# FFN up-projection pairs as Strassen's seven products, with the down units of one chunk between the products of the next

## The chip, the cores and the metric

One core of one Trainium2 chip runs the whole program. The metric is the device time of one execution in microseconds. PE is TensorE (matmul), DVE VectorE, ACT ScalarE, POOL GpSimd, SP SyncE, which here issues the loads of weights.

## What is computed

One step of a two-layer encoder on 576 tokens: 512 of a prompt and 64 of a sample. Layer 0 mixes with attention and a linear recurrence, layer 1 with chunked spatial gating. Each mixer and each FFN is followed by x <- LN(alpha x + f(x)) over 1024 features. The change lies in the gated FFN of both layers:

```
def conv_ffn(x, conv_state, w_up, conv_w, conv_b, w_down):
    hc, new_state = causal_dwconv(x @ w_up, conv_state, conv_w, conv_b)   # width 3, along the tokens
    g, u = jnp.split(hc, 2, axis=-1)
    return (jax.nn.gelu(g) * u) @ w_down, new_state
```

`w_up` is 1024 x 5632 (g and u of 2816 each, 22 tiles of 128), `w_down` 2816 x 1024, all float32.

## The kernel before

**Layout.** x lies feature-major: 8 tiles of 128 features by 576 tokens, worked on in two halves of 288 (`HALF`). Every large product is made of float32r parts, each operand split exactly into high and low. `triplet` (L288) issues three matmuls for one inner tile of 128: high by high (L293), high by low of the activations (L294), low by high (L295). The normalised x is held as `xh` and `xl`, the hidden tiles as `hh` and `hl`.

**Weight stream.** `units` lists all weight tiles in order of use. `dma_next` (L134 to L143) has SP load one into one of four `raw` buffers, at most four ahead of the splits. A split (`split_part`, L162) is an ACT copy to the high part (L164) and a DVE subtraction for the low part (L165), into one of two sets of four slots, A and B.

**FFN before** (`ffn`, L1039). The 22 column pairs are worked through in three chunks of 8, 7 and 7 (`CHUNKS`). Per pair j there are two up units, g and u: 8 inner tiles x 3 matmuls x 2 halves = 48 matmuls each. `up_post` evacuates the banks on ACT (L1056, L1058, L1059), POOL makes the base of the convolution (L1062), DVE its other two taps (L1064), then gelu on ACT (L1069), multiply on DVE (L1074) and the split of the hidden tile (`h_split`, L801 on ACT, L802 on DVE). After a chunk come its eight down units, which add into x (`z_post`, L1095, L1097). The first four up units of an FFN run one half of the tokens after the other (`first_group`), while the layer norm of the second half is still made by hooks at fixed places in the first half's sweep: statistics (L422 on PE, L432 a power on POOL), broadcast (L439), centering, scaling (L462 on POOL) and low parts (L471 on DVE).

**Order.** Each engine takes its instructions in program order. The DMAs of SP and POOL stand in these orders too. What is issued early in the code is early on its engine, whether its inputs are there or not.

Of the kernel before, what the change touches and what calls it, by code (L numbers as in the profile page):

```python
# [25 lines left out]
D = 1024  # L26
# [13 lines left out]
CHUNKS = ((0, 8), (8, 15), (15, 22))  # L40
# [7 lines left out]
class Unit:  # L48
    def __init__(self, src, slot, nk, width=128):
        self.src, self.slot, self.nk, self.width = src, slot, nk, width  # L50
        self.raw = self.hi = self.lo = None
        self.parts = ((0, nk),)


@with_exitstack
def stream_step(ctx, tc, I, O):
# [21 lines left out]
    units = []  # L78

    def wunit(w, off, ncols, c0, k0, nk, slot):  # L80
        u = Unit(dram(w, off + k0 * 128 * ncols + c0, [[ncols, 128], [128 * ncols, nk], [1, 128]]), slot, nk)
        units.append(u)
        return u

    def vunit(w, ncols, c0, k0, slot, width=512):
        u = Unit(dram(w, k0 * 128 * ncols + c0, [[ncols, 128], [128 * ncols, 2], [1, width]]), slot, 2, width)
        units.append(u)
        return u

    def weight_list():  # L90
# [11 lines left out]
        def ffn_units(layer):  # L102
            n = 0
            up, down = {}, {}
            for c, (j0, j1) in enumerate(CHUNKS):
                for j in range(j0, j1):
                    for s in range(2):
                        up[j, s] = wunit(I["ffn_w_up"], layer * D * 2 * DFF, 2 * DFF, s * DFF + 128 * j, 0, 8,
                                         "BA"[(n // 4) % 2])
                        n += 1  # L110
                for m in range(8):
                    down[c, m] = wunit(I["ffn_w_down"], layer * DFF * D, D, 128 * m, j0, j1 - j0,
                                       "BA"[(n // 4) % 2])
                    n += 1
            Fs.append((up, down))
# [15 lines left out]
    st = {"dma": 0, "split": 0}  # L131
    live = {"A": 0, "B": 0}

    def dma_next():  # L134
        if st["dma"] >= len(units) or st["dma"] >= st["split"] + 4:
            return False
        u = units[st["dma"]]
        st["dma"] += 1
        u.raw = raws.tile([128, 1040], FT, name="raw")
        for k0, k1 in u.parts:  # L140
            nc.sync.dma_start(u.raw[:, k0 * u.width:k1 * u.width].rearrange("p (k c) -> p k c", k=k1 - k0),
                              u.src[:, k0:k1])
        return True  # L143

    def split_next():
        if st["split"] >= st["dma"]:
            return False
        u = units[st["split"]]
        p = wpool[u.slot]
        if p is None or live[u.slot] >= 4:  # L150
            return False
        st["split"] += 1
# [1217 lines left out]
```

## Time and profile before

| | |
|---|---|
| three timed executions | 1321.57, 1319.81, 1320.72 us (median 1320.72) |
| span of the profiled execution | 1319.8 us |
| PE, DVE, ACT, POOL busy | 98%, 58%, 37%, 30% of the span |
| mean granted clock of PE | 0.987 |
| matmuls | 9567 |
| DMA | 113.8 MB, mean 86 GB/s |

The profile is one execution; the page gives no time for it other than its span, which lies 0.9 us under the median of the timed ones. A busy share is a mean over the whole program, and an engine that is half idle can still be the one that another waits for at a given place.

### The profile page before, as it was taken

The page shows a single profiled execution, that of the slowest core. Times are in us where ns is not written, and L with a number is a line of the kernel's source. Part 1 is how long each engine was busy: PE and PEld are TensorE (multiplying, and loading weights), DVE is VectorE, ACT ScalarE, POOL GpSimd, SP SyncE. Part 2 cuts the span into 40 slices and gives each one's busy share as a digit, 9 for nine tenths or more (in the row PEclk, how much of TensorE's full clock was granted, in tenths as well). Part 3 has the DMA queues.
Part 4 walks back from the last instruction along what each step waited for, and adds up shares of the span by engine and source line. Part 5 has one row for each costly group of instructions (what it writes and reads, how often), then busy time and mean ns, then how long its engine had stood idle before and what let it go on. Part 6 is the DMA issues. An engine that isn't in the chain of part 4 may idle for free. (4 is left out here: it accounts for less than half of the span.)

```text
span 1319.8 us, 23538 instructions
## 1 busy us (share of the span) xinstructions
PE 1290.8 (98%) x9567; PEld 1256.0 (95%) x9567; DVE 768.4 (58%) x1294; ACT 483.1 (37%) x936; POOL 398.2 (30%) x603
## 2 busy tenths in 40 slices
PE   8999999999999999999999998999999999999995
PEld 8999888999999999999999788999999999999995
DVE  4557777777543555355564348777653465445556
ACT  4553554445421332234334242444431233223331
POOL 3322222763200221022183025565320122012234
PEclk9999999999999999999999998999999999999997
DMA  9316221314232223322312412314323222322112
GB/s 234 113 33 199 79 84 41 97 47 144 83 96 80 74 74 94 97 75 71 94 38 68 139 50 73 96 33 128 113 80 96 78 66 81 97 86 64 43 36 72
DMA packets 192017, 113.80 MB, mean 86 GB/s; under 512 B 4221, under 2 KB 184733, under 8 KB 191909
## 3 DMA queue, kind: packets, MB, share of 16 engines
q1 hardware_dynamic: 191300, 111.95, 28.9%
q8 instruction: 75, 1.23, 0.4%
q0 software_dynamic: 608, 0.35, 0.2%
q14 instruction: 34, 0.27, 0.1%
HBM read 107.07 MB, written 5.22 MB: 85 GB/s over the span
## 5 line engine op out<-in xcount | busy, mean ns | idle before, releaser
L293 PE MATMUL mm<-xh,whiA 128*128 128x288 f32 (+2 forms) x960 | 285.4, 297 | 1.6 <-ACT xh L512 1.6
L295 PE MATMUL mm<-xh,wloA 128*128 128x288 f32 (+2 forms) x960 | 283.7, 296 | 1.4 <-DVE wloA L165 1.4
L294 PE MATMUL mm<-xl,whiA 128*128 128x288 f32 (+2 forms) x960 | 283.9, 296 | 0.5 <-DVE xl L513 0.5
L1064 DVE SCALAR_TENSOR_TENSOR y<-hb,vecF,y 128x578 f32<-128x578 f32 x176 | 146.5, 834 | 193.3 <-POOL y L1062 190.2
L1062 POOL TENSOR_SCALAR y<-hb,vecF 128x578 f32<-128x578 f32 x88 | 81.6, 928 | 557.5 <-issue 546.2
L293 PE MATMUL mm<-xh,whiB 128*128 128x288 f32 x768 | 226.5, 295 | 0.0
L295 PE MATMUL mm<-xh,wloB 128*128 128x288 f32 x768 | 226.4, 295 | 0.0
L294 PE MATMUL mm<-xl,whiB 128*128 128x288 f32 x768 | 226.2, 295 | 0.0
L165 DVE TENSOR_TENSOR wloA<-raw,whiA 128x1024 fp32r<-128x1024 f32 (+3 forms) x118 | 141.3, 1211 | 110.4 <-ACT whiA L164 109.8
L293 PEld LDWEIGHTS mm<-xh,whiA 128*128 128x128 f32 x960 | 181.3, 189 | 2.5 <-ACT xh L512 1.8
L295 PEld LDWEIGHTS mm<-xh,wloA 128*128 128x128 f32 x960 | 181.1, 189 | 1.6 <-DVE wloA L165 1.6
L294 PEld LDWEIGHTS mm<-xl,whiA 128*128 128x128 f32 x960 | 181.2, 189 | 0.7 <-DVE xl L513 0.7
L293 PE MATMUL mm<-hh,whiA 128*128 128x288 f32 (+2 forms) x576 | 171.5, 298 | 0.1
L294 PE MATMUL mm<-hl,whiA 128*128 128x288 f32 (+2 forms) x576 | 170.4, 296 | 0.8 <-DVE hl L1202 0.7
L295 PE MATMUL mm<-hh,wloA 128*128 128x288 f32 (+2 forms) x576 | 170.0, 295 | 0.0
L164 ACT ACTIVATE whiA<-raw 128x1024 fp32r<-128x1024 f32 (+3 forms) x118 | 119.5, 1025 | 133.7 <-PE mm L294 81.4
L293 PEld LDWEIGHTS mm<-xh,whiB 128*128 128x128 f32 x768 | 144.1, 188 | 0.0
L294 PEld LDWEIGHTS mm<-xl,whiB 128*128 128x128 f32 x768 | 144.1, 188 | 0.0
L295 PEld LDWEIGHTS mm<-xh,wloB 128*128 128x128 f32 x768 | 144.1, 188 | 0.0
L294 PEld LDWEIGHTS mm<-hl,whiA 128*128 128x128 f32 x576 | 108.8, 189 | 1.2 <-DVE hl L1202 1.2
L293 PEld LDWEIGHTS mm<-hh,whiA 128*128 128x128 f32 x576 | 108.8, 189 | 0.4 <-DVE x L361 0.4
L295 PEld LDWEIGHTS mm<-hh,wloA 128*128 128x128 f32 x576 | 108.6, 189 | 0.0
(330 smaller groups left out, 2374.1 us busy)
## 6 DMA issues: line engine op xcount, KB each, us to landing
raw<-in_ffn_w_up_dram SPq DMA_DIRECT2D x88, 512.0 KB
raw<-in_ffn_w_down_dram SPq DMA_DIRECT2D x32, 448.0 KB
raw<-in_ffn_w_down_dram SPq DMA_DIRECT2D x16, 512.0 KB
raw<-in_w_in_o_dram SPq DMA_DIRECT2D x16, 512.0 KB
raw<-in_w_in_e_dram SPq DMA_DIRECT2D x14, 512.0 KB
raw<-in_w_out_e_dram SPq DMA_DIRECT2D x8, 512.0 KB
raw<-in_w_out_o_dram SPq DMA_DIRECT2D x8, 512.0 KB
biasb<-nbd SPq DMA_DIRECT2D x4, 832.0 KB
```

Source lines behind the costliest of these rows:

```text
L164: ACT.activation(u.hi[:, c], u.raw[:, c], AF.Copy)
L165: DVE.tensor_sub(u.lo[:, c], u.raw[:, c], u.hi[:, c])
L293: PE.matmul(o, wh, h[:, k, a:b], start=first, stop=False)
L294: PE.matmul(o, wh, l[:, k, a:b], start=False, stop=False)
L295: PE.matmul(o, wl, h[:, k, a:b], start=False, stop=last)
L1062: POOL.tensor_scalar(y, t[:, 2:580], V[:, 88 + ct:89 + ct], V[:, 132 + ct:133 + ct], op0=OP.mult, op1=OP.add)
L1064: DVE.scalar_tensor_tensor(y, t[:, q:q + 578], V[:, 44 * q + ct:44 * q + ct + 1], y, op0=OP.mult, op1=OP.add)
```

## The change

The FFN of both layers is rewritten. The pairs j = 0 and 1 stay plain. From j = 2 on, g and u of a pair are one 2x2 block product: the inner dimension in two halves of 512, the columns g and u, the tokens in two halves of 288. Strassen's form in seven products of 12 matmuls (4 inner tiles x 3) takes the place of eight, so 84 matmuls for a pair instead of 96, 20 pairs per layer. In exchange there are sums of operands: of weights, per pair (`pair_sums` on POOL; `pair_split` copies the sum to a high part and its negative, on ACT, and an accumulating DMA from POOL's queue adds the sum to the latter, which leaves the low part), of x, once per FFN (`x_sums`, `x_sum3`, `x_split3`), and of products, per pair on DVE.

`CHUNKS` becomes seven (2, 3, 3, 3, 3, 3 and 5 tiles). Hidden tiles live in a ring of five. The eight down units of a chunk run inside the windows of the next chunk: `window` issues the seven products with two or three calls of `d_run` after or between them, while the convolution, gelu and split of the pair before (`pend`) and the weights of the pair after (`nxt`) are made. A window at a chunk's start has two units, the next two have three, the last two of an FFN none. Down weights come through one buffer `draw`, loaded by SP and split one unit ahead. The base of the convolution moves from POOL to ACT. For the FFN's start the weight sums of pair 2 are issued inside the first half's sweep, before the hooks of the layer norm. The last chunk's down units and the final layer norm are put in another order (`ffn_tail`, `fin_early`).

```diff
-CHUNKS = ((0, 8), (8, 15), (15, 22))
+CHUNKS = ((0, 2), (2, 5), (5, 8), (8, 11), (11, 14), (14, 17), (17, 22))
+RING = 5
...
+    BL = {"B11": (0, 0), "B21": (4, 0), "B22": (4, H2), "t3": (0, H2)}
...
+            def base(self, s):
+                ct = s * NJ + self.j
+                ACT.activation(self.y[s], self.t[s][:, 2:580], AF.Identity, scale=V[:, 88 + ct:89 + ct],
+                               bias=V[:, 132 + ct:133 + ct])
...
+        def x_sums():
+            for e in range(2):
+                lo, hi = x[:, 2 * e:2 * e + 2], x[:, 4 + 2 * e:6 + 2 * e]
+                s = tmp[e].raw[:, :2 * H2].rearrange("p (k c) -> p k c", k=2)
+                for name, eng, a, b in (("t1", DVE, lo[:, :, H2:], lo[:, :, :H2]), ("t2", DVE, hi[:, :, H2:], s),
+                                        ("t4", POOL, s, hi[:, :, :H2])):
+                    eng.tensor_sub(s, a, b)
+                    ACT.activation(tb[name, 0][e], s, AF.Copy)
+                    DVE.tensor_sub(tb[name, 1][e], s, tb[name, 0][e])
...
+        def prod(bk, w, off, name):
+            hi, lo = w
+            o = bk[:, :H2]
+            for k in range(4):
+                c = slice(off + 128 * k, off + 128 * k + 128)
+                PE.matmul(o, hi[:, c], operand(name, 0, k), start=k == 0, stop=False)
+                PE.matmul(o, hi[:, c], operand(name, 1, k), start=False, stop=False)
+                PE.matmul(o, lo[:, c], operand(name, 0, k), start=False, stop=k == 3)
...
+        def pair_sums(g):
+            r1, r2 = g.one.raw, g.two.raw
+            POOL.tensor_add(r2[:, b_], r2[:, a_], r2[:, b_])
+            POOL.tensor_sub(r2[:, a_], r1[:, a_], r2[:, a_])
+            POOL.tensor_sub(r1[:, a_], r2[:, b_], r1[:, a_])
+            POOL.tensor_sub(r1[:, b_], r1[:, b_], r1[:, a_])
+
+        def pair_split(g, i):
+            hi, lo = (t[:, :1024] for t in g.w[i])
+            r = (g.two if i == 2 else g.one).raw[:, :1024]
+            ACT.activation(hi, r, AF.Copy)
+            ACT.activation(lo, r, AF.Copy, scale=-1.0)
+            POOL.dma_start(lo, r, accum_op=OP.add)
+            if i == 3:
+                free_raw(2)
...
+        def d_split():
+            i = dn["split"]
+            if i < dn["load"] and i < dn["run"] + 2:
+                dn["split"] += 1
+                u = down[dq[i]]
+                u.hi, u.lo = (t[:, 512:512 + u.nk * 128] for t in S[i % 2][1])
+                ACT.activation(u.hi, draw[:, :u.nk * 128], AF.Copy)
+                DVE.tensor_sub(u.lo, draw[:, :u.nk * 128], u.hi)
+                d_load()
...
+        def window(g, nxt, pend, nd, first):
...
+            prod(b1, w1, 0, "B11")
+            ACT.activation(p1, b1[:, :H2], AF.Copy)
+            if nxt:
+                pair_hi(nxt)
+            pend.conv(1)
+            pend.conv(0)
+            b0 = mmbank()
+            prod(b0, w1, 512, "B21")
+            if nxt:
+                pair_lo(nxt, 1)
+            DVE.tensor_add(me.t[0][:, 2:2 + H2], b0[:, :H2], p1)
+            if nxt:
+                pair_lo(nxt, 0)
+            pend.gelu()
+            pend.mul()
+            pend.split()
+            if nxt:
+                pair_sums(nxt)
+            b5 = mmbank()
+            prod(b5, w2, 0, "t4")
+            if nd > 2:
+                d_run()
+            if nxt:
+                pair_split(nxt, 2)
+            b4 = mmbank()
+            prod(b4, w3, 512, "t1")
+            b3 = mmbank()
+            prod(b3, w3, 0, "t3")
+            if nd > 2:
+                d_run()
+            if nxt:
+                pair_split(nxt, 3)
+            b2 = mmbank()
+            prod(b2, w4, 0, "t2")
+            DVE.tensor_add(u2, b2[:, :H2], p1)
...
+            prod(b6, w4, 512, "B22")
...
+            for _ in range(1 if nd > 2 else nd):
+                d_run()
...
+            hooks = prev.hooks(1, (13, 15, 17, 20))
...
+            hooks[2] = begin
+            hooks[5] = lambda: pair_sums(g)
+            hooks[8] = lambda: pair_split(g, 2)
+            hooks[11] = lambda: pair_split(g, 3)
+            sweep(us, 0, xh, xl, post, outer=True, hooks=hooks)
...
+                pend = window(up[j], up.get(j + 1), pend, (2, 3, 3, 0, 0)[j - j0], j == 2)
```

**Order on POOL at the start of an FFN.** Before, the last rows ahead of the layer norm's power step (L432) are four memsets:

```order
L1044 MEMSET hb_3159 128x2
L1044 MEMSET hb_3160 128x2
L1044 MEMSET hb_3161 128x2
L1044 MEMSET hb_3162 128x2
L432 TENSOR_TENSOR sb<-sb,nhalf 96x3 [waits DVE_49]
L451 TENSOR_TENSOR x<-x,cs_2680 128x288 [waits Activation_49]
L451 TENSOR_TENSOR x<-x,cs_2680 128x288 [waits Pool_49]
L451 TENSOR_TENSOR x<-x,cs_2680 128x288
L462 TENSOR_SCALAR x<-x,vec 128x288 [waits Activation_49] x8
```

Now (the power step is L448, L1198 to L1201 are the pair sums, L1208 the accumulating DMAs, L1084 the state columns of the convolution):

```order
L1084 COPY hb_3162<-vecF_136 128x2
L1198 TENSOR_TENSOR raw<-raw 128x512 [waits DMAHW2_49,DMAHW5_49,DMAHW1_49,DMAHW6_49,DMAHW0_49,DVE_49]
L1199 TENSOR_TENSOR raw<-raw 128x512 [waits DMAHW4_49,Pool_49]
L1200 TENSOR_TENSOR raw<-raw 128x512 [waits DMAHW2_49,DMAHW0_49,DMAHW3_49,DVE_49,Pool_49]
L1201 TENSOR_TENSOR raw<-raw 128x512 [waits Pool_49]
L1208 DMA wloA<-raw 128x1024 [waits DMASW3_49,Activation_49]
L1208 DMA wloA<-raw 128x1024 [waits DMASW4_49,Activation_49,Pool_49]
L448 TENSOR_TENSOR sb<-sb,nhalf 96x3 [waits DVE_49]
L467 TENSOR_TENSOR x<-x,cs_2682 128x288 [waits Activation_49]
L467 TENSOR_TENSOR x<-x,cs_2682 128x288 x2
L478 TENSOR_SCALAR x<-x,vec 128x288 [waits Activation_49] x8
```

Four sums and two DMA issues, which wait for ACT, now stand between the memsets and the power step.

**Order on SP.** Before, the queue holds one kind of load, each waiting for the split that frees its buffer:

```order
L141 DMA raw<-in_ffn_w_down_dram 128x8x128 [waits DMAHW3_49,DVE_49]
L141 DMA raw<-in_ffn_w_up_dram 128x8x128 [waits DMAHW4_49,DVE_49]
L141 DMA raw<-in_ffn_w_up_dram 128x8x128 [waits DMAHW5_49,DVE_49]
L141 DMA raw<-in_ffn_w_up_dram 128x8x128 [waits DMAHW6_49,DVE_49]
L141 DMA raw<-in_ffn_w_up_dram 128x8x128 [waits DMAHW7_49,DVE_49]
```

Now, at the window of j = 4 and the crossing into the third chunk (L168 loads up weights, L1237 a down unit; DMASW names the accumulating DMAs of POOL):

```order
L168 DMA raw<-in_ffn_w_up_dram 128x8x128 [waits DMASW1_49,Pool_49]
L168 DMA raw<-in_ffn_w_up_dram 128x8x128 [waits DMASW2_49,Activation_49,Pool_49]
L1237 DMA draw<-in_ffn_w_down_dram 128x3x128 [waits DMAHW6_49,DVE_49]
L168 DMA raw<-in_ffn_w_up_dram 128x8x128 [waits DMAHW2_49,DMASW3_49,DMAHW3_49,Activation_49,Pool_49]
L168 DMA raw<-in_ffn_w_up_dram 128x8x128 [waits DVE_49,DMASW4_49,Activation_49,Pool_49]
L1237 DMA draw<-in_ffn_w_down_dram 128x3x128 [waits DMAHW1_49,DVE_49]
L1237 DMA draw<-in_ffn_w_down_dram 128x3x128 [waits DMAHW4_49,DVE_49]
```

The first two of these rows, and again the fourth and fifth, are up weights that wait for accumulating DMAs; the last two are the down loads of the window with two units, and both now come behind the second pair of up weights.

**Order on ACT at a crossing.** At the end of the window of j = 5, which has two units, and the start of that of j = 6 (L1206 and L1207 are `pair_split`, L1245 the split of a down unit, L1091 the base of the convolution, L1275 the copy of the first product, L1186 and L1187 the high parts of the next pair, L1101 gelu, L823 the high hidden tile):

```order
L1206 ACTIVATE whiB<-raw 128x1024 [waits Pool_49]
L1207 ACTIVATE wloB<-raw 128x1024 [waits DMASW2_49]
L1091 ACTIVATE y<-hb_3160,vecF_136 128x578 [waits DVE_49,Activation_49]
L1245 ACTIVATE whiB<-draw 128x384 [waits DMAHW3_49]
L1245 ACTIVATE whiA<-draw 128x384 [waits DMAHW6_49,PE_49]
L1091 ACTIVATE y<-hb_3159,vecF_136 128x578 [waits DVE_49]
L1275 ACTIVATE y<-mm 128x288 [waits PE_49,Activation_49]
L1186 ACTIVATE whiA<-raw 128x512 [waits DMAHW2_49]
L1187 ACTIVATE whiA<-raw 128x1024 [waits DMAHW1_49]
L1101 ACTIVATE y<-y 128x578 [waits DVE_49]
L823 ACTIVATE hh<-y 128x576 [waits DVE_49]
L1245 ACTIVATE whiB<-draw 128x384 [waits DMAHW7_49,Activation_49]
```

The splits of down units stand in line with the work of the windows: two at the window's end, ahead of the next window's base and of the first product's copy, one behind gelu and the high hidden tile.

## Rows read from the trace of the kernel before

**Rows 1.** The page: the span, and the busy time of all engines.

```profile
span 1319.8 us, 23538 instructions
...
PE 1290.8 (98%) x9567; PEld 1256.0 (95%) x9567; DVE 768.4 (58%) x1294; ACT 483.1 (37%) x936; POOL 398.2 (30%) x603
```

**Rows 2.** Windows, engines by stretch: busy time (instructions), granted clock, DMA share, GB/s.

```profile
400.00:440.00 40.00, 40.00 (x304) 40.00 (x304) 15.61 (x21) 10.69 (x18) 4.75 (x12) 1.00 0.23 67
...
277.08:289.70 12.62, 12.62 (x98) 12.62 (x97) 9.52 (x16) 8.31 (x16) 11.55 (x16) 1.00 0.30 84
```

**Rows 3.** Groups by line and form: busy us, mean ns, idle before and releasers.

```profile
L1064 DVE SCALAR_TENSOR_TENSOR y<-hb,vecF,y 128x578 f32<-128x578 f32 x176 | 146.5, 834 | 193.3 <-POOL y L1062 190.2
...
L165 DVE TENSOR_TENSOR wloA<-raw,whiA 128x1024 fp32r<-128x1024 f32 x94 | 116.2, 1253 | 87.6 <-ACT whiA L164 87.6
...
L164 ACT ACTIVATE whiA<-raw 128x1024 fp32r<-128x1024 f32 x94 | 97.7, 1054 | 132.8 <-PE mm L294 81.4 <-PE mm L688 44.4 <-PE mm L711 6.3
...
L802 DVE TENSOR_TENSOR hl<-y,hh 128x576 fp32r<-128x576 f32 x44 | 33.4, 758 | 33.1 <-ACT hh L801 33.1
L1058 ACT ACTIVATE hb<-mm 128x224 f32<-128x224 f32 x88 | 31.4, 356 | 100.7 <-PE mm L295 100.6
L1074 DVE TENSOR_TENSOR y<-y 128x512 f32<-128x512 f32 x44 | 30.4, 692 | 1.8
L801 ACT ACTIVATE hh<-y 128x576 fp32r<-128x576 f32 x44 | 30.2, 686 | 153.7 <-DVE y L1075 153.7
L1069 ACT ACTIVATE y<-y 128x578 f32<-128x578 f32 x44 | 30.1, 683 | 21.8 <-DVE y L1064 21.8
...
L1059 ACT ACTIVATE hb<-mm 128x64 f32<-128x64 f32 x88 | 19.2, 218 | 0.0
...
L363 DVE TENSOR_TENSOR x<-x,mm 128x288 f32<-128x288 f32 x40 | 17.2, 446 | 3.5 <-PE mm L295 3.5
...
L797 POOL TENSOR_TENSOR gg<-gg,rr 128x512 f32<-128x512 f32 x4 | 7.2, 1791 | 0.0
```

**Rows 4.** Timeline at the first FFN's start: start, us, operation; POOL, then DVE.

```profile
271.40 0.86 POOL L432 TENSOR_TENSOR sb<-sb,nhalf 96x3 f32<-96x3 f32 x1 [2.83 <-DVE sb L431]
...
269.04 0.45 DVE L391 TENSOR_TENSOR a<-a,sq 128x288 f32<-128x288 f32 x1
...
282.07 0.46 DVE L471 TENSOR_TENSOR xl<-x,xh 128x288 fp32r<-128x288 f32 x1 [0.41 <-POOL x L462]
```

**Rows 5.** One line at a time: POOL's L797, ns; L732's DMA; L531's landing.

```profile
L797 POOL TENSOR_TENSOR gg<-gg,rr x4: 1085/1940/2199, 98.1 to 104.9; 128x512 f32<-128x512 f32 x4
...
L732 POOL DMA_DIRECT2D out_dram<-ls x1: 825/825/825, 96.7 to 96.7; - x1
...
DMA to landing us min/median/max: 2.2/2.2/2.2
...
DMA to landing us min/median/max: 6.6/6.6/6.6
```

**Rows 6.** Timeline of SP's queue: a load of up weights.

```profile
303.55 6.20 SPq L141 DMA_DIRECT2D raw<-in_ffn_w_up_dram  x4
```

**Rows 7.** Windows of 1 us behind that issue: clock, DMA share, GB/s.

```profile
304.00:305.00 1.00, 1.00 0.14 40
305.00:306.00 1.00, 1.00 0.94 268
306.00:307.00 1.00, 1.00 1.05 310
```

**Rows 8.** Timeline of PE at a wait, and the window behind it.

```profile
694.28 0.64 PE L422 MATMUL aux<-mones,s1r 128*96 128x1 f32 x6 [1.10 <-DVE s1r L407]
...
696.00:700.00 4.00, 4.00 (x22) 3.98 (x21) 2.83 (x9) 0.91 (x2) 3.18 (x4) 0.57 0.01 2
```

**Rows 9.** One line at a time: DVE's multiply and POOL's addition beside it.

```profile
L1193 DVE TENSOR_TENSOR mt<-mt,x x8: 691/1188/1475, 805.2 to 826.0; 128x512 f32<-128x512 f32 x8
...
L1198 POOL TENSOR_TENSOR x<-xh,xl x8: 1417/1810/1824, 806.1 to 827.4; 128x576 f32<-128x576 f32 x8
```

More of the change, by code (lines that the diff above doesn't have):

```diff
@@ L52, in __init__ @@
         self.parts = ((0, nk),)
+        self.slots = list(range(nk))
+class Pair:
+    def __init__(self, one, two, j):
+        self.one, self.two, self.j = one, two, j
+        self.w = None
 @with_exitstack
@@ new lines, in z_post, with d_load @@
+        def z_post(c, m, half, bk):
+            a, b = HALF[half]
+            xm = x[:, m, a:b]
+            if c == 0:
+                DVE.scalar_tensor_tensor(xm, xm, ALPHA, bk[:, :H2], op0=OP.mult, op1=OP.add)
+            else:
+                DVE.tensor_add(xm, xm, bk[:, :H2])
+        dq = [(c, m) for c in range(len(CHUNKS) - 1) for m in range(8)]
+        dn = {"load": 0, "split": 0, "run": 0}
+        def d_load():
+            i = dn["load"]
+            if i < len(dq) and i == dn["split"]:
+                dn["load"] += 1
+                u = down[dq[i]]
+                nc.sync.dma_start(draw[:, :u.nk * 128].rearrange("p (k c) -> p k c", k=u.nk), u.src)
@@ new lines, in ffn @@
+        pend, tes = first_pairs()
+        last = len(CHUNKS) - 1
+        dl = [down[last, m] for m in range(8)]
+        for c, (j0, j1) in enumerate(CHUNKS):
+            for j in range(max(j0, 2), j1):
+                pend = window(up[j], up.get(j + 1), pend, (2, 3, 3, 0, 0)[j - j0], j == 2)
+                if j == NJ - 2:
+                    for m in range(3):
+                        plain_split(dl[m], S[0][m])
+        plain_split(dl[3], S[0][3])
+        pend.all(False)
+        plain_split(dl[4], S[1][0])
@@ new lines, in ffn @@
+        tes.close()
+        open_ln()
+        cut["h"] = norm.halves
+        banks = kouter(dl[0:3], hh, hl, norm.post, npost=2)
+        live["A"] -= 3
+        for m in range(5, 8):
+            plain_split(dl[m], S[1][m - 4])
+        pump(3)
+        bk = auxbank()
+        sT = ytile()[:88, :256].rearrange("p (q c) -> p q c", q=2)
+        for q in range(2):
+            PE.transpose(bk[:88, 128 * q:128 * q + 128],
+                         stage[:, 2 * q:2 * q + 2, :].rearrange("p a u -> p (a u)"), ident)
@@ L1141, in stream_step @@
     up_mask = op.tile([128, 128], FT, name="up_mask")
[L1142 removed]
+    jo = op.tile([128, 128], I32, name="jo")
+    POOL.iota(jo, pattern=[[1, 128]], base=0, channel_multiplier=-1)
+    DVE.tensor_scalar(up_mask, jo, 0.0, None, op0=OP.is_ge)
     def vo_post(sw):
```

400 lines of the change are left out of this document (254 added, 146 removed).

## The prediction

> **What bounds the kernel now.** I read the page's engine line first: TensorE is busy for 98% of the span [rows 1]. Then the engines by stretch: inside the FFN it is busy without a gap at a granted clock of 1.00, 304 matmuls in 40 us, so 131.6 ns for one of 288 columns [rows 2]. The chain of waits on the page adds nothing; it follows only the last microseconds. So the FFN is as long as its matmuls, and a matmul removed is worth 131.6 ns as long as everything that feeds TensorE still comes in time. VectorE is at 58% and ScalarE at 37%: there is room in the mean, but each engine works in order, and a wait on one row holds the rows behind it. The prediction is therefore a sum of one sure gain and of waits, each found by following one chain.
>
> **The gain.** 20 pairs per layer need 84 instead of 96 matmuls: 2 x 20 x 12 = 480 x 0.1316 = **-63.2 us**. A product of 12 matmuls takes 1.58 us, a down unit of three inner tiles 18 x 0.1316 = 2.37. A window of seven products is 11.06 us, with two down units 15.8, with three 18.2. Work per window with three units, by the groups' means [rows 3]: VectorE four conv steps of 0.83, low parts 0.63 (half of 1.25) and 1.25, multiply and low of the hidden tile 0.69 + 0.76, some seven additions and six down additions near 0.45, three splits near 0.5: about 14 of 18.2. Throughput is no bound; the order is.
>
> **Start of each FFN (+14.6 for both).** POOL now does four pair sums and two DMA issues before the power step of the layer norm, and TensorE's broadcast that waits for that step stands where it stood. Before, VectorE's last addition ended at 269.49, the step at 272.26 [rows 4]. Now the low part ends at 269.49 + 0.63 = 270.1. A sum of 128x512 with two inputs is bounded by 1.09 (the least of the same form) and 1.94 (its median) [rows 5]; I take 1.44, halfway between 1.09 and the mean 1.79 [rows 3, 5]. Four end at 275.9; two ScalarE copies of 1.05 wait for them: 278.0; the DMA issue costs at most 0.83 [rows 5], taken 0.7, the step 0.86: 279.6. That is 7.3 us late, while TensorE has nothing else. Bounds 5.6 to 9.0 per layer.
>
> **First pair window (+36.8).** Shifted by 7.3, the last low part ends at 282.53 + 7.3 = 289.8 [rows 4] and the plain sweeps at 289.70 + 7.3 = 297.0 [rows 2]. The sums of x run in series on one scratch tile per half: five VectorE steps of 0.76, three ScalarE copies of 0.69, one POOL step of 1.44, 7.3 twice: 304.4. Behind them in order: evacuations 2 x (0.36 + 0.22), a conv base 0.68, four conv steps 3.3, multiply 0.69, high 0.69 and low 0.76: 311.7; the difference t3 twice 0.76, then 0.69 + 0.76: 314.6 [rows 3]. TensorE wants t3 after four products, at 303.3: **11.3** late. The first down unit wants the low part of hidden tile 1: 315.4 + 3.3 + 0.63 + 0.45 + 1.25 + 0.69 + 0.69 + 0.76 = 323.2 against 319.3: **3.9**. The second has its split behind the pair splits on ScalarE: 319.3 + 5.8 + 2.1 + 0.8 = 328.0 against 324.8: **3.2**. 18.4 per layer; bounds 13 to 23.
>
> **Six chunk crossings per layer (+55.2).** The window with two units (A) is the weak one. From its start: conv ends at 3.8, low parts at 4.4 and 6.1, sums at 4.4 + 5.8 = 10.2, the last copies at 12.3. Then POOL issues an accumulating DMA of 512 KB inside SBUF, and SP's next weight load waits for it. The trace shows no such DMA. The nearest rows: a small POOL DMA out of SBUF lands in 2.2 us, a load on the same queue in 6.6 [rows 5]; the weight load of 512 KB starts to move about 1.3 us after its issue at some 290 GB/s, 1.85 us [rows 6, 7]. Bounds: 2.2 with nothing for the data, 6.6 + 2 x 1.85 = 10.3 with reading and writing apart. I take **5**, nearer 2.2 + 1.85, because that small DMA also starts from SBUF and the long rows resemble it more. So SP goes on at 17.3 and the next draw load, *behind* two weight loads in SP's order, lands at 17.3 + 1.3 + 1.85 + 0.65 + 0.2 = 21.3, the last number for SP's step. ScalarE and VectorE have the split of that draw ahead of all work of the next window (B), which begins at 15.8. B's first down unit is wanted at 20.5 and has its split at 22.3: +1.8. Its second has its split on ScalarE behind gelu and the high part of the pending pair: VectorE starts conv at 22.4 + 0.5, ends 26.2, low parts and one addition 28.5, multiply and high 29.9, split 31.2 at the latest; without a stall it is wanted at 26.0. I count 4.6 per crossing for both, the 0.6 that is left being within what the short additions are uncertain by: 12 x 4.6 = 55.2. Bounds: 0.4 (DMA 2.2, sums 1.09) to 9.9 (DMA 10.3): 5 to 119. All other windows have a draw loaded ahead of the weight loads, or a whole window of slack: nothing.
>
> The Trainium skill, "DMA: Bandwidth & Descriptors", section "Anatomy of one DMA — SWDGE (gpsimd) path", fits such a DMA as 2.0 us + bytes / 436e3, which for 512 KB makes an estimate of 3.2 us in place of 5; by it each crossing would cost 1.8 less and the time would be some 22 us lower, 1363; the 2.2 us of the small DMA agree with its fixed part, and no run here shows the large one.
>
> **End of each FFN (+11).** The split of the third of the last down units waits for its load, which stands behind the last accumulate: it lands some 9.4 us into the last window and holds ScalarE (1.5 us for the sixth bank), then the last hidden tile is late for the first down units, which cover 72 x 0.1316 = 9.5 us of it (4.0). 5.5 per layer, bounds 2 to 10.
>
> **Clock.** A wait of 1.10 us was followed by a granted clock of 0.57 for 4 us, that is 1.7 us lost [rows 8]. Some twelve crossings could pay that: 0 to 20; I take 10. The moved masks, the ring of five hidden tiles and the new final order cost nothing: each is a few instructions beside a busy TensorE.
>
> **Sum:** -63.2 + 14.6 + 36.8 + 55.2 + 11 + 10 = +64.4. The profiled execution's span is 1319.8, 0.9 under the median of 1320.72: 1384.2 + 0.9 = **1385**.
>
> **Rivals.**
> - *The waits are mostly covered, faster.* If the accumulate lands in 2.2 and sums take 1.09, crossings cost 5, the start 11, the first window 26, the end 4, the clock nothing: -63.2 + 46 = -17, **1304**; with every wait covered 1257. It turns on whether the draw lands before window B's start, which needs both. For it: a POOL DMA of 2.2 us is in the trace. Against: the start and the first pair window lose 37 alone even at their least.
> - *VectorE and POOL hold each other up, slower still.* A multiply of 128x512 took 0.69 us at best and 1.475 beside POOL's addition of x [rows 9]. If low part, multiply and hidden low (1.25 + 0.69 + 0.76 = 2.7) are serialised with the pair sums, some 1.6 us more fall on the chain of each window A and of most Bs, 11 x 1.6 x 2 = 35: **1420**. It decides where the sums run beside VectorE work with two SBUF inputs, in every window. The Trainium skill, "SBUF — State Buffer", section "SBUF: two separate sides", says just this, an exclusive lock on a shared port while a VectorE operation with two SBUF inputs meets a POOL operation that reads SBUF; the 1.475 agrees.
> - *Gain and waits cancel.* Between the first rival and the forecast lies no change; no mechanism picks it.
>
> **How the numbers follow.** Forecast 0.58, covered 0.27, mutual hold-up 0.12, cancel 0.03. What this measurement can tell from no change is 0.2%, 2.6 us. So faster 0.27, same 0.03, slower 0.70. The low bounds of all terms make about -17, the high ones +140 with 20 of clock on top; the range leaves out the far ends of both, and takes in the covered case and the hold-up: 1290 to 1450. The slower cases alone lie at 1340 to 1450.
>
> **What would show it.** Right: 480 fewer matmuls of 288 columns; POOL's power step about 7 us after VectorE's copy; a gap of about 11 us on TensorE ahead of the third left operand t3 in each FFN; in every window after a crossing ScalarE and VectorE standing at the draw's split with SP's weight load behind a POOL DMA. Wrong: TensorE without gaps through the crossings, or accumulates that land within 3 us of issue, then the time falls to the first rival; a step of the sums above 1.9 us beside VectorE points to the second.

## The result, and the profile after

The changed kernel takes **1589.5 us** (median of four, 1587.3 to 1592.4) against 1320.3 us for the kernel before in the same rounds: ratio 1.204, interval 1.203 to 1.206. The forecast was 1385, the range 1290 to 1450: the sign was right, the size far outside.

The page of the kernel after, against [rows 1]:

```profile
span 1588.9 us, 23653 instructions
...
PE 1320.7 (83%) x9087; PEld 1267.9 (80%) x9087; DVE 1058.5 (67%) x1875; ACT 660.0 (42%) x1064; POOL 595.6 (37%) x672
```

TensorE has 480 matmuls fewer and is busy for *longer*, and idle (span less busy time) for 268.2 us where it was 29.0. So the 269.1 us of extra span split in two: +239.2 of idle time, and +29.9 of busy time, which is the -63.2 of the removed matmuls plus, by difference, 93.1 for slower ones. The clock of the profile after:

```profile
core 0: 1588.9 us, clock 0.917
```

Before, it was 0.987. **Who TensorE waits for**, over the whole program (columns: us in total, times, longest):

```profile
PE aux L311 <- DVE x L1226: 113.2, 30, 6.4
PE aux L311 <- DVE x L1224: 28.4, 8, 7.0
PE aux L311 <- ACT y L1275: 26.3, 10, 4.2
PE aux L455 <- POOL sb L448: 15.2, 2, 8.2
PE mm L1177 <- ACT xh L1163: 11.7, 2, 6.0
PE aux L438 <- DVE s1r L423: 9.5, 4, 5.8
PE aux L390 <- ACT y L1394: 6.8, 1, 6.8
PE aux L311 <- ACT hh L823: 6.3, 2, 3.3
...
PE mm L1177 <- ACT y L1275: 4.8, 2, 3.2
...
PE mm L311 <- DVE y L1308: 4.4, 2, 2.4
PE aux L312 <- DVE hl L824: 2.7, 4, 0.8
```

The first three rows are the down units inside the windows: 167.9 us in 48 waits. L1224 and L1226 are the additions of a down unit into x, which free the bank that the next unit wants. They run for 0.45 us each; they are late because VectorE reaches them late. In the third row TensorE waits for a place in ScalarE's order, the copy L1275, which stands behind the split of a draw. Two reasons for the lateness stand in the trace. First, **the draw**. The waits of ScalarE, and SP's queue before one of them:

```profile
ACT whiA L1245 <- DMA draw<-in_ffn_w_down_dram: 142.4, 23, 11.0
```

```profile
544.22 3.57 SPq L168 DMA_DIRECT2D raw<-in_ffn_w_up_dram  x2
547.89 6.04 SPq L1237 DMA_DIRECT2D draw<-in_ffn_w_down_dram  x2
```

```profile
552.41 0.52 ACT L1245 ACTIVATE whiA<-draw 128x384 fp32r<-128x384 f32 x1 [10.14 <-DMA draw<-in_ffn_w_down_dram]
552.84 0.86 ACT L1091 ACTIVATE y<-hb,vecF 128x578 f32<-128x578 f32 x1
```

ScalarE stands for 10.14 us at the split of a draw that SP could only ask for at 547.89, behind two loads of up weights; the base of the next pair's convolution (L1091) stands behind it. Second, **VectorE's operations are long**. Groups by line and form of VectorE, then of POOL:

```profile
L1105 DVE TENSOR_TENSOR y<-y 128x512 f32<-128x512 f32 x44 | 71.5, 1624 | 2.4 <-ACT y L1101 2.3
...
L1106 DVE TENSOR_TENSOR y<-y 128x64 f32<-128x64 f32 x44 | 50.8, 1154 | 0.0
L824 DVE TENSOR_TENSOR hl<-y,hh 128x576 fp32r<-128x576 f32 x44 | 47.8, 1087 | 33.0 <-ACT hh L823 33.0
L1194 DVE TENSOR_TENSOR wloB<-raw,whiB 128x1024 fp32r<-128x1024 f32 x20 | 43.4, 2169 | 0.0
```

```profile
L1199 POOL TENSOR_TENSOR raw<-raw 128x512 f32<-128x512 f32 x40 | 84.3, 2107 | 3.1
L1200 POOL TENSOR_TENSOR raw<-raw 128x512 f32<-128x512 f32 x40 | 63.8, 1596 | 3.1
L1198 POOL TENSOR_TENSOR raw<-raw 128x512 f32<-128x512 f32 x40 | 53.6, 1339 | 306.2 <-DVE wloA L1192 151.2 <-DVE wloB L1192 149.8 <-DMA draw<-in_ffn_w_down_dram 5.2
L1201 POOL TENSOR_TENSOR raw<-raw 128x512 f32<-128x512 f32 x40 | 51.1, 1278 | 3.1
```

The multiply took 692 ns before and the hidden tile's low part 758 [rows 3]; now 1624 and 1087. One window on VectorE and POOL:

```profile
486.70 2.16 DVE L1194 TENSOR_TENSOR wloA<-raw,whiA 128x1024 fp32r<-128x1024 f32 x1
488.78 1.75 DVE L1105 TENSOR_TENSOR y<-y 128x512 f32<-128x512 f32 x1
490.45 1.28 DVE L1106 TENSOR_TENSOR y<-y 128x64 f32<-128x64 f32 x1
492.48 1.13 DVE L824 TENSOR_TENSOR hl<-y,hh 128x576 fp32r<-128x576 f32 x1 [0.75 <-ACT hh L823]
...
494.01 0.81 DVE L1226 TENSOR_TENSOR x<-x,aux 128x288 f32<-128x288 f32 x2
```

```profile
486.50 1.28 POOL L1198 TENSOR_TENSOR raw<-raw 128x512 f32<-128x512 f32 x1 [14.83 <-DVE wloA L1192]
487.86 2.13 POOL L1199 TENSOR_TENSOR raw<-raw 128x512 f32<-128x512 f32 x1
490.06 1.59 POOL L1200 TENSOR_TENSOR raw<-raw 128x512 f32<-128x512 f32 x1
491.73 1.27 POOL L1201 TENSOR_TENSOR raw<-raw 128x512 f32<-128x512 f32 x1
```

The four sums run from 486.50 to 493.00, the four VectorE rows from 486.70 to 493.61, side by side. TensorE's row at the end of that chain, and the stretch behind it:

```profile
494.59 0.58 PE L311 MATMUL aux<-hh,whiB 128*128 128x288 f32 x1 [6.37 <-DVE x L1226]
```

```profile
494.00:496.00 2.00, 1.41 (x6) 1.44 (x7) 0.81 (x3) 0.75 (x1) 0.87 (x1) 0.50 0.26 77
496.00:498.00 2.00, 2.00 (x11) 2.00 (x11) 0.54 (x2) 1.10 (x2) 0.00 (x0) 0.56 0.94 189
498.00:500.00 2.00, 2.00 (x17) 2.00 (x17) 0.83 (x3) 1.32 (x2) 0.14 (x1) 1.00 0.87 191
```

After the gap of 6.37 us the granted clock is 0.50 and 0.56, the lower level (1.2 GHz), as in [rows 8], and the row counts 11 matmuls in 2 us instead of 17. Such stretches stand behind many of the gaps, not behind all: behind the gap of 3.24 us that ended at 482.42 the granted clock is 1.00.

### The profile page after: what moved, and what is told of

The parts are those of the page before. It is cut to its first block, busy times and chain, and to the rows that moved or that the text cites. A ratio compares the mean times of both kernels' runs of the same rounds, so it can differ in the third digit from the quotient of the medians.

```text
span 1588.9 us, 23653 instructions
## 1 busy us (share of the span) xinstructions
PE 1320.7 (83%) x9087; PEld 1267.9 (80%) x9087; DVE 1058.5 (67%) x1875; ACT 660.0 (42%) x1064; POOL 595.6 (37%) x672
## 4 chain that ended last, share of the span: by engine, by line
DVE 36%; PE 25%; issue 14%; DMA 9%; ACT 9%; POOL 5%; SPq 0%; DVEq 0%; ACTq 0%; POOLq 0%
DVE y L1097 6%; DVE y L1105 4%; DMA draw<-in_ffn_w_down_dram 3%; DVE y L1106 3%; PE mm L311 3%; PE mm L312 3%; PE mm L313 3%; DVE wloB L1194 3%; DMA wloB<-raw 2%; DVE wloA L1194 2%; PE aux L311 2%; DMA wloA<-raw 2%; POOL x L478 2%; PE aux L313 2%; PE aux L312 2%
## 5 line engine op out<-in xcount | busy, mean ns | idle before, releaser
L311 PE MATMUL aux<-hh,whiB 128*128 128x288 f32 x272 | 95.3, 350 | 107.7 <-DVE x L1226 88.8
L1198 POOL TENSOR_TENSOR raw<-raw 128x512 f32<-128x512 f32 x40 | 53.6, 1339 | 306.2 <-DVE wloA L1192 151.2
L311 PEld LDWEIGHTS aux<-hh,whiB 128*128 128x128 f32 x272 | 62.7, 231 | 112.8 <-ACT whiA L1206 37.8
L311 PE MATMUL aux<-hh,whiA 128*128 128x288 f32 x272 | 88.3, 325 | 66.5 <-ACT y L1275 26.3
L823 ACT ACTIVATE hh<-y 128x576 fp32r<-128x576 f32 x44 | 30.1, 684 | 209.6 <-DVE y L1106 209.6
L311 PEld LDWEIGHTS aux<-hh,whiA 128*128 128x128 f32 x272 | 56.1, 206 | 71.8 <-ACT y L1275 28.4
L1091 ACT ACTIVATE y<-hb,vecF 128x578 f32<-128x578 f32 x88 | 75.9, 863 | 79.4 <-DVE hb L1311 79.2
L1177 PE MATMUL mm<-xh,whiA 128*128 128x288 f32 x320 | 95.8, 299 | 11.7 <-ACT xh L1163 11.7
L1177 PE MATMUL mm<-xh,whiB 128*128 128x288 f32 x320 | 96.7, 302 | 4.8 <-ACT y L1275 4.8
L311 PE MATMUL mm<-hh,whiA 128*128 128x288 f32 (+2 forms) x304 | 94.7, 311 | 6.1 <-DVE y L1308 4.4
L311 PE MATMUL mm<-xh,whiA 128*128 128x288 f32 (+2 forms) x320 | 97.0, 303 | 1.8 <-ACT xh L534 1.8
L313 PE MATMUL mm<-xh,wloA 128*128 128x288 f32 (+2 forms) x320 | 95.4, 298 | 1.5 <-DVE wloA L202 1.5
L1178 PE MATMUL mm<-xl,whiB 128*128 128x288 f32 x320 | 96.3, 301 | 0.0
L1178 PE MATMUL mm<-xl,whiA 128*128 128x288 f32 x320 | 95.8, 299 | 0.4 <-DVE xl L1164 0.4
L1179 PE MATMUL mm<-xh,wloB 128*128 128x288 f32 x320 | 96.0, 300 | 0.0
L312 PE MATMUL mm<-xl,whiA 128*128 128x288 f32 (+2 forms) x320 | 95.6, 299 | 0.5 <-DVE xl L535 0.5
L1179 PE MATMUL mm<-xh,wloA 128*128 128x288 f32 x320 | 95.6, 299 | 0.0
L312 PE MATMUL mm<-hl,whiA 128*128 128x288 f32 (+2 forms) x304 | 92.7, 305 | 0.8 <-DVE hl L1504 0.7
```

The lines of the kernel that those rows point to most:

```text
L311: PE.matmul(o, wh, h[:, k, a:b], start=first, stop=False)
L312: PE.matmul(o, wh, l[:, k, a:b], start=False, stop=False)
L313: PE.matmul(o, wl, h[:, k, a:b], start=False, stop=last)
L1091: ACT.activation(self.y[s], self.t[s][:, 2:580], AF.Identity, scale=V[:, 88 + ct:89 + ct], bias=V[:, 132 + ct:133 + ct])
L1177: PE.matmul(o, hi[:, c], operand(name, 0, k), start=k == 0, stop=False)
L1178: PE.matmul(o, hi[:, c], operand(name, 1, k), start=False, stop=False)
```

## The experiments

Each was run beside the kernel before, which took 1320.2 to 1321.4 us. Runs 1 to 12 are single executions; the four of the changed kernel lie up to 5.1 us apart, so a difference of some 5 us (runs 4, 7, 9) or 1 us (run 6) can't be told from none by the time alone. Two theories were set against each other: the waits come from *VectorE and POOL holding each other up*, or from *the order of the queues* (draws behind up weights, splits behind other splits). Runs 1, 2 and 4 change one thing each in the changed kernel, and run 3 adds one to run 2. From run 6 to run 11 each edit stands on top of the run before it.

**1. Sums late.** A one-column copy on POOL that reads the hidden tile's low part puts the pair sums behind VectorE's work.

```diff
             if nxt:
+                POOL.tensor_copy(gate[:, 0:1], hl[:, pend.j % RING, 575:576].bitcast(FT))
                 pair_sums(nxt)
```

> One POOL copy of a single column is put ahead of the pair sums, so that they start only when VectorE has written the low part of the hidden tile. POOL and VectorE do the same work, only not at the same time. Theory 'mutual hold-up' (POOL's sums and VectorE's operations with two SBUF inputs stretch each other): low part of 1024 back from 2.16 to about 1.25 us, the multiplies from 1.62 and 1.15 to 0.69 and 0.22, the low hidden tile from 1.09 to 0.76, POOL's second sum from 2.1 to 1.3. Theory 'order only' (the operations are long for another reason): these durations stay. For the time: the hidden tile is done some 3 us earlier but the sums end some 3 us later, so the gaps at the second unit of the windows with three units shrink (6.4 to 3, 2.4 to 0) and the two at the crossing grow (3.1 and 3.3 to about 6): 1590 within 25 by my reading, under 1540 if the hold-up alone bounds the windows.

Measured 1561.5, 28 less. The same groups of VectorE as above:

```profile
L824 DVE TENSOR_TENSOR hl<-y,hh 128x576 fp32r<-128x576 f32 x44 | 33.4, 759 | 33.0 <-ACT hh L823 33.0
L1105 DVE TENSOR_TENSOR y<-y 128x512 f32<-128x512 f32 x44 | 30.1, 684 | 2.4 <-ACT y L1101 2.3
L1194 DVE TENSOR_TENSOR wloA<-raw,whiA 128x1024 fp32r<-128x1024 f32 x20 | 24.3, 1216 | 0.2
...
L1106 DVE TENSOR_TENSOR y<-y 128x64 f32<-128x64 f32 x44 | 9.6, 217 | 0.0
```

All four durations are back: the stretch of the VectorE rows is shown to be due to the sums beside them. But the time hardly is: 133 us of VectorE's busy time went (1058.5 to 925.7; 3.5 us for each of the 38 windows with sums), and 28 us of the program. That is a net figure, since the copy also makes the sums, and what waits for them, later.

**2. Up weights late.** The two loads of a pair's weights are given to SP at the window's end, behind the draws (the added False keeps `pair_split` from freeing the buffers).

```diff
-                pair_split(nxt, 3)
+                pair_split(nxt, 3, False)
...
             for _ in range(1 if nd > 2 else nd):
                 d_run()
+            if nxt:
+                free_raw(2)
```

> SP's two loads of up weights, which wait for the accumulating DMAs, are issued at the end of a window, behind the loads of down units, instead of in front of them. Nothing else moves. Theory 'queue' (the crossing is long because the down load stands behind loads that wait for the accumulate): ScalarE's 10 us wait for the draw goes, the 3.3 us gap of TensorE at the first unit behind a crossing goes and the 6.4 us gap at the second falls to the 2.4 of the other windows; with the clock some 9 us per crossing, 12 crossings: about 1480. Theory 'hold-up' as the sole cause: the gaps stay, 1590.

Measured 1531.8: 58 less, half of what was hoped. ScalarE's wait for draws in the row above fell from 142.4 to 89.0 us, not to nothing.

**3. Also the split early.** As 2, with the next unit's split at the window's start.

```diff
             pend.conv(0)
+            d_split()
             b0 = mmbank()
```

> As the run before, and in each window the split of the unit that runs second is issued at the window's start, behind the convolution, instead of behind gelu, hidden tile and pair splits. Theory 'order': the gap of 3.1 us at the second unit of the window with two units falls to about 1, which the bank of the first unit needs; the gaps of 2.4 at the second unit of the other windows stay near 2, since the additions into x, which free the banks, still stand behind the hidden tile on VectorE: about 1450. If the split's place is not what these units wait for, the time is that of the run before.

Measured 1505.6: another 26, a third of what was hoped. ScalarE's waits for draws are down to 7.0 us.

**4. The layer norm first.** The sums and splits of pair 2 behind the layer norm's hooks at the FFN's start.

```diff
-            hooks[5] = lambda: pair_sums(g)
-            hooks[8] = lambda: pair_split(g, 2)
-            hooks[11] = lambda: pair_split(g, 3)
+            hooks[21] = lambda: pair_sums(g)
+            hooks[24] = lambda: pair_split(g, 2)
+            hooks[27] = lambda: pair_split(g, 3)
```

> At the FFN's start the sums and splits of pair 2 are issued behind the layer norm's hooks instead of ahead of its power step. The gap of 8.2 us at TensorE's broadcast in the first sweep goes in both FFNs, with the clock after it some 11 us each: 1590 - 20 = about 1570. The first pair's last weights land later, at some 295 us; if that is too late for its products, up to 8 us per FFN come back there.

Measured 1595.1: no gain. The gap of 8.18 us went and two others came. On VectorE and on TensorE of this run:

```profile
292.51 0.76 DVE L1149 TENSOR_TENSOR raw<-x 128x576 f32<-128x576 f32 x1 [8.60 <-DMA wloA<-raw]
```

```profile
290.15 0.40 PE L311 MATMUL mm<-xh,whiB 128*128 128x288 f32 x1 [4.32 <-ACT hb L1331]
```

Now the sums of x wait for the accumulating DMA (their scratch tile is one of its buffers), and the evacuations wait behind the pair splits. The wait was moved: the start is not one late row. That it is too much work for three engines in one place is a reading, not shown here.

**5. Three together** (1 and 3).

> The three edits so far that each gave time, together: sums behind the hidden tile, up loads behind the down loads, the split of the second unit at the window's start. Theory 'two causes' (order of splits and queues, and the mutual hold-up, each lengthens the same chain): without the hold-up the additions that free the banks come 3 us earlier, so the gaps of 3.2 and 2.7 at the second unit of the three-unit windows go, and the 1.5 in the two-unit windows stay: 1505 - 13 windows x 2 x (3 + 1 for the clock) = about 1400. Theory 'one cause' (the hold-up was only a loss where a split waited behind it): no more than the 28 us that the first edit gave, about 1480.

Measured 1478.5, the higher of the two values: the gains of runs 1 and 3 simply add (28 + 84 = 112; measured 111), and 157 us are left over the kernel before. Taken alone this speaks for "one cause". But holding the sums back has its price here: ScalarE's waits for draws, 7.0 us in run 3, are back at 94.4:

```profile
ACT whiB L1246 <- DMA draw<-in_ffn_w_down_dram: 68.2, 32, 3.7
ACT whiA L1246 <- DMA draw<-in_ffn_w_down_dram: 26.2, 19, 3.0
```

**6. Units apart.** On top of 5: the first down unit ahead of the pending pair's low part and of the sums; of two units, one ahead of the last product.

```diff
-            pend.split()
...
+            ACT.activation(hh[:, pend.j % RING, :], pend.y[1][:, :T], AF.Copy)
             b5 = mmbank()
             prod(b5, w2, 0, "t4")
             if nd > 2:
                 d_run()
+            pend.split(True)
...
             me.base(1)
+            if nd == 2:
+                d_run()
             b6 = mmbank()
```

> As the run before; the first unit of a three-unit window is issued ahead of the low part of the pending hidden tile, so its additions come earlier on VectorE, and in a two-unit window one product is put between the two units, so that the additions of the first run beside it. Theory 'banks' (what is left in the windows is a unit that waits for the additions of the unit before): the 1.5 us gaps at the twelve two-unit windows go, 12 x (1.5 + up to 1 for the clock) = some 20 to 30 us less than the run before. If VectorE is full, the time stays.

Measured 1479.4: nothing. ScalarE still waits 97.4 us for draws, so the splits were as late as in run 5.

**7. The first pair reordered.** Sums of x for both halves side by side in tiles of their own, pair sums behind the sweep, t3 earlier.

```diff
+            for lo, hi, s in X:
+                DVE.tensor_sub(s, lo[:, :, H2:], lo[:, :, :H2])
+            part("t1")
...
-            hooks[5] = lambda: pair_sums(g)
+            pair_sums(g)
+            x_sums()
```

> As the run before; at the FFN's start the weight sums of pair 2 come behind the layer norm, and the sums of x are made for both halves side by side in spare tiles that wait for no accumulating DMA, the third difference ahead of the first hidden tile. Theory: the 8.2 us gap at the broadcast goes without the new gaps that the fourth run showed, where the sums of x waited for the accumulate and the banks' evacuation behind the pair splits; VectorE's 20 us of work before the first down unit leaves a gap of about 5. So about 13 us of gap and 8 of clock less per FFN, some 35 to 45 us less than the run before. If the time falls by under 10, the start only moves its wait, as in the fourth run.

Measured 1474.6: 5 less where 35 to 45 were expected, a miss. The sums of x now ran beside the pair sums: the first two of them took 3.62 us together, against 1.4 for the next two.

**8. Queues spread.** Both pair splits behind the second unit; the up weights behind the next window's early draw (`pay` frees the buffers that are owed).

```diff
             d_split()
+            pay()
...
-            if nxt:
-                pair_split(nxt, 2)
...
             if nxt:
+                pair_split(nxt, 2)
                 pair_split(nxt, 3, False)
...
-            if nxt:
-                free_raw(2)
+            owed[0] = 2 if nxt else 0
```

> As the run before, with two orders more: the pair splits of a three-unit window come behind its second unit instead of in front of it on ScalarE, and SP's two up loads come behind the down load that the next window's early split issues. Theory 'order' (the 1.5 to 3.0 us gaps that are left in every window are ScalarE standing at a draw behind up loads, or at pair splits ahead of a unit's split, with VectorE's additions behind it): some 9 us of gaps per three windows go, 6.5 such groups per FFN, and part of the clock: 1475 - 100 = about 1375. Theory 'VectorE full' (some 16 of 18 us of work per window leave no room): at most 30 less.

Measured 1445.9: 29 less, within what the theory "VectorE full" allowed. ScalarE's waits for draws stay at 100.3 us; run 10 shows that VectorE was not full.

**9. The first pair again.** POOL's differences t4 ahead of its waiting DMA; the copies out of the banks ahead of the pair splits.

```diff
-            pair_split(g2[0], 2)
             for lo, hi, s in X:
                 POOL.tensor_sub(s, s, hi[:, :, :H2])
...
+            def rest():
+                pair_split(g2[0], 2)
```

> As the run before; at the FFN's start POOL's two differences of x come ahead of the accumulating DMA, and the copies of the first pair's banks ahead of the pair splits on ScalarE. If the 5.5 and 2.8 us gaps in the first pair window stand behind these two orders, 4 to 8 us less per FFN, so 10 to 15 in all; if they are VectorE's own work (some 20 us between the layer norm and the first down unit), nothing.

Measured 1440.6: 5 less, neither of the two values.

**10. Splits ahead.** The down unit's split and the convolution's base ahead of the second pair split, whose copies wait for the late sums.

```diff
                 pair_split(nxt, 2)
-                pair_split(nxt, 3, False)
+            if nd > 2:
+                d_split()
...
             me.base(1)
             if nd == 2:
                 d_run()
+                d_split()
+            if nxt:
+                pair_split(nxt, 3, False)
```

> As e9_first_pair_again; in every window the split of the next window's first unit comes on ScalarE ahead of the second pair split and of nothing that waits, and the base of the convolution ahead of that pair split too. Theory 'order': VectorE's 1.3 to 3 us of waits for ScalarE at a window's end and at its early draw go, and with them TensorE's gaps of 0.8 to 2.9 per window: 20 windows x 1.5 x 2 = 60, with the clock up to 90 less: 1350 to 1385. Theory 'VectorE full': at most 20 less.

Measured **1377.8**: 63 less, as expected. ScalarE's waits for draws fell from 100.3 to 10.4 us. A stretch of 80 us in the middle of the first FFN, in run 5 and then in run 10 (columns as in [rows 2]):

```profile
450.00:530.00 80.00, 68.27 (x494) 67.22 (x494) 47.55 (x94) 38.59 (x54) 28.55 (x44) 0.97 0.59 131
```

```profile
450.00:530.00 80.00, 78.09 (x588) 77.66 (x588) 59.36 (x120) 43.66 (x62) 36.37 (x49) 1.00 0.62 142
```

In the same 80 us 94 more matmuls are done: TensorE is busy for 78 of 80 us at the full clock. The windows *can* run nearly without gaps, so that the seven products pay inside them.

**11. End of the FFN.** On top of 10: the last chunk's five windows carry 2, 2, 2, 1 and 1 units instead of 2, 3, 3, 0 and 0, one split of the last down units comes inside the last window (`first` now marks that window), and the next layer's weights are split later. In the last two windows the units read places of the ring that later hidden tiles have overwritten: the same instructions, other values.

```diff
             pend.mul()
+            if first:
+                plain_split(dl[2], S[0][2])
...
-                pend = window(up[j], up.get(j + 1), pend, (2, 3, 3, 0, 0)[j - j0], j == 2)
+                pend = window(up[j], up.get(j + 1), pend, ((2, 2, 2, 1, 1) if j0 == 17 else (2, 3, 3))[j - j0], j == NJ - 1)
```

> As the run before; the last chunk's windows carry 2, 2, 2, 1, 1 units instead of 2, 3, 3, 0, 0, the third of the last down units is split inside the last window, and the next layer's weights are split behind the shift instead of ahead of it. The 3.3, 1.1 and 2.4 us gaps at the FFN's end and the 6.9 us one behind it (where ScalarE stood at a weight load) go; with the clock 15 to 20 us in the first FFN, less in the second: 20 to 35 less than the run before. If they only move, as in the fourth run, under 10.

Measured 1358.0: 20 less.

**12. Sums early again.** Run 11 without the copy of run 1; its last two windows too read overwritten places.

```diff
-                POOL.tensor_copy(gate[:, 0:1], hl[:, pend.j % RING, 575:576].bitcast(FT))
                 pair_sums(nxt)
```

> As e11_end_of_ffn, but without the one-column copy that held back POOL's sums: they run beside VectorE's low part and multiplies again. Theory 'hold-up': these operations stretch as in the changed kernel (2.16, 1.62, 1.15, 1.09 us) and TensorE's gaps of some 3 us per three-unit window come back: 30 to 60 us more. If order alone was the matter, the time is the same, or less, since the sums end earlier.

Measured 1423.1: **65 more** than run 11. VectorE's groups are stretched again (in run 11 they stand at 686, 219, 758 and 1217 ns):

```profile
L1103 DVE TENSOR_TENSOR y<-y 128x512 f32<-128x512 f32 x44 | 71.7, 1630 | 2.4 <-ACT y L1099 2.3
L1104 DVE TENSOR_TENSOR y<-y 128x64 f32<-128x64 f32 x44 | 50.5, 1148 | 0.0
L1109 DVE TENSOR_TENSOR hl<-y,hh 128x576 fp32r<-128x576 f32 x40 | 45.0, 1124 | 13.9 <-ACT hh L1318 13.5
...
L1213 DVE TENSOR_TENSOR wloA<-raw,whiA 128x1024 fp32r<-128x1024 f32 x20 | 42.5, 2125 | 0.2
```

Net, the hold-up is worth 28 us while the draws are late anyway and 65 once they are not, which "one cause" (28 and no more) does not allow. Both theories hold; neither explains the result alone.

**13. Start and end.** On top of 10, the ring kept whole: both ends reordered.

```diff
-            hooks[2] = begin
+            begin()
+            hooks[8] = lambda: sums12(g)
+            hooks[16] = lambda: pair_split(g, 2)
...
-                pend = window(up[j], up.get(j + 1), pend, (2, 3, 3, 0, 0)[j - j0], j == 2)
+                pend = window(up[j], up.get(j + 1), pend, ((2, 3, 2, 1, 0) if j0 == 17 else (2, 3, 3))[j - j0], j == NJ - 1)
```

> As e10_splits_ahead, with the FFN's two ends put in another order: at the start the first two weight sums of pair 2 come ahead of the power step and the others behind the layer norm, all sums of x on VectorE, the third difference's split ahead of the first hidden tile; at the end the last chunk's windows carry 2, 3, 2, 1, 0 units, the third of the last down units is split inside the last window, and the next layer's weights one at a time between the units. Theory 'order everywhere': the 14 us of gaps at the start fall to about 5 and the 14 to 20 at the end to about 8, with the clock 1378 - 2 x 20 = 1330 to 1345. Theory 'VectorE is the bound at the start' (some 24 us of its work between the layer norm and the first down unit): only the end gains, 1355 to 1365.

Measured 1358.1 (1356.7 to 1358.6), ratio 1.028, interval 1.026 to 1.030. The best version of the study, still 37.5 us slower than the kernel before. By its page TensorE is idle for 98.9 us, 70 more than before, and busy for 1258.0, 32.8 less: the 63.2 gained, 30 given back at the lower clock. VectorE in the first pairs:

```profile
286.00:317.00 31.00, 21.36 (x146) 20.68 (x144) 25.16 (x35) 18.07 (x32) 5.92 (x10) 0.88 0.25 64
```

VectorE is busy for 25.2 of 31 us and its pauses are short waits, at most 1.51 us, nearly all for ScalarE within one chain: this stretch goes by the chain through VectorE, as one of the two theories had it. At the first FFN's end one gap of 12.78 us stands where run 10 had two of 6.87 and 4.69, so nothing was gained at that place. In it VectorE first waits 6.85 us for POOL, and then the weight splits that I put one by one between units come between the layer norm's operations. A version without them was not tried.

## Why the prediction was wrong

| term | forecast | measured in the changed kernel |
|---|---|---|
| 480 matmuls fewer | -63.2 | -63.2 |
| start of each FFN | +14.6 | +15.2 |
| first pair window | +36.8 | +20.7, and 2.4 per FFN of the next row |
| down units in windows | +55.2 | +167.9 |
| end of each FFN | +11 | about +20 |
| clock | +10 | +93.1 (by difference) |

The waits are sums of rows of the waits table: the start is L455; the first window L1177 for xh, L311 for hh and L312; the units the first three rows; the end L390, L1177 for y, L311 for y at L1308, and two short rows that are not shown. The measured waits are 224 of the 239 us of extra idle time; the rest lies in the layer norms (L438, 2.6 us before) and in small waits.

**What was right.** The matmuls. The accumulating DMA of 512 KB, taken at 5, landed in 5.4 (the median of the profile's page). By the fit of the Trainium skill, "DMA: Bandwidth & Descriptors", section "Anatomy of one DMA — SWDGE (gpsimd) path", the estimate was 3.2; here the measurement decides. The start came to 15.2 where 14.6 were forecast (8.18 and 7.03 for 7.3 each): POOL's power step (L448) was forecast to end at 279.6, 7.3 us late; it began at 279.51. The crossing's mechanism (the draw behind two up loads behind an accumulate) stands in the trace as described.

**The first pair window** was over-priced for a reason that teaches something. The third left operand was forecast for 314.6; TensorE's first matmul with it started here:

```profile
314.44 0.61 PE L1177 MATMUL mm<-xh,whiA 128*128 128x288 f32 x1 [5.69 <-ACT xh L1163]
```

The chain was right at its steps too: the last low part ended at 289.55 (forecast 289.8), the sums of x at 304.71 (304.4), the hidden tile at 312.68 (311.7). But the wait is 5.69 and not 11.3, because TensorE itself came at 308.75 and not at 303.3. Its way there from the restart (columns: length, PE busy, clock, DMA share, GB/s):

```profile
281.20:308.75 27.55, 27.55 (x191) 0.91 0.22 58
```

191 matmuls at 131.6 ns make 25.1 us, so 2.4 of the 5.4 us are the lower clock behind the gap at the start; 0.9 are the longer gap, and the rest, by elimination, my place for the end of the plain sweeps. Where a fixed chain ends last, a slow TensorE on the way there costs nothing more: the loss stands under clock instead of under waits.

**The step that failed** is the price of the windows: "I count 4.6 per crossing" and "All other windows have a draw loaded ahead of the weight loads, or a whole window of slack: nothing." From one crossing to the next the middle of the FFN shows four gaps:

```profile
482.42 0.37 PE L311 MATMUL aux<-hh,whiA 128*128 128x288 f32 x1 [3.24 <-ACT y L1275]
...
516.97 0.37 PE L311 MATMUL aux<-hh,whiA 128*128 128x288 f32 x1 [2.44 <-DVE x L1226]
543.37 0.37 PE L311 MATMUL aux<-hh,whiB 128*128 128x288 f32 x1 [3.10 <-DVE x L1226]
```

The first is the draw, forecast at 1.8; the second is that of 6.37 shown above (the additions behind VectorE's stretched chain), for which the rest of the forecast's 4.6 stood, 2.8; that of 2.44 (the same additions, one window on) and that of 3.10 (between the two units of the window with two) at nothing: 15.2 us where 4.6 were forecast, and 167.9 in all where 55.2 were. Two things were left out.

1. *Durations from an empty neighbourhood.* Low part, multiply, small multiply and hidden low stood at 1.25, 0.69, nothing and 0.76. Beside the sums they take 2.1, 1.62, 1.15 and 1.09: the 64-column multiply, not even in my sum, is the worst (217 ns alone, 1154 here): in the window shown it starts at 490.45 and ends 0.08 us behind POOL's third sum. The second rival named this and priced it at 1.6 us per window and 35 us in all, with a chance of 0.12; run 1 shows 3.5 per window, and run 12 prices it at 65. The Trainium skill, "SBUF — State Buffer", section "SBUF: two separate sides", gives the rule, an exclusive lock for the whole of an operation when a VectorE operation with two SBUF inputs meets a POOL operation that reads SBUF; runs 1 and 12 agree with it.
2. *Slack that was not there.* VectorE's mean load of 14 in 18.2 us per window was read as room. But in each window the order puts the next unit's split, the additions that free a bank, and the next pair's convolution behind whatever is late, so a delay is handed on from window to window. Runs 2, 3, 8 and 10, which only reorder, took 58, 26, 29 and 63 us off, and in run 10 the windows run nearly without gaps on the same engines.

**The clock term** was sized at some twelve waits of 1.7 us each, and halved. There were 48 waits in the windows alone, and more at both ends of the FFNs: 93 us for 239 of extra waiting, about 40 us for each 100. At that rate the 117.6 us of waits that were forecast would have cost 46 of clock, and the sum would have been 1421, inside the range. With the measured waits of the table and the clock at 10 it would have been 1491, outside. So the price of the windows is what failed first, and the clock followed it.

Of the rivals, "mostly covered" is out: accumulates of 5.4 us, no crossing without a gap. The mutual hold-up was the true direction, but at 1420 it still kept my crossing prices and my clock. Even with order and hold-up mended as far as these runs went, the form loses: 63 us gained, against 70 of waits and 30 of clock that are left (run 13). Whether a better order at the FFNs' ends would turn this is not shown.

## What to carry to other kernels

When a kernel that keeps TensorE busy at 98% is given less matmul work and more work elsewhere, price the other engines' operations by rows in which their *new* neighbours run, and follow each in-order queue over several iterations, not one: a mean load of 77% is no slack if a late item hands its delay on. Count a loss of clock with the gaps that are forecast (here 93 us with 239 of them, and 30 with 70 in run 13). When an experiment that removes a shown cost gives little, it may be covered by a second wait: take both away, then put the first back (runs 1 and 12: 28 and 65 us for the same copy).

## What was not expected of the hardware

A VectorE operation of 64 columns took as long beside POOL's sums (1154 ns) as one of 576 (1087). Both are means over 44 operations, of which 38 run in windows with sums; in the window shown they took 1.28 and 1.13 us. So what an operation pays there does not go by its own size, and small operations with two inputs lose most for theirs. POOL pays as well, unevenly: the second and third sums took 2107 and 1596 ns, the first and fourth 1339 and 1278; in run 1, with those VectorE rows out of the way, all four take 1282 to 1331.
